# A hybrid block on one core: last accumulators in a bank of their own, a norm's factor left in PSUM, transposes behind the sums, side pairs dealt anew

## The chip, the core and the metric

The kernel runs on one core of a Trainium2 chip. TensorE is called PE here (PEld is its weight load), VectorE DVE, ScalarE ACT, GpSimd POOL and SyncE SP. The metric is the device time of one execution in microseconds (us); a lower one is better.

## What is computed

One layer of a diffusion block on 256 tokens of width 2048, with 256 context tokens, in fp32:

```python
mod = (silu(c) @ ada_w[l] + ada_b[l])
sh1, sc1, g1, sh2, sc2, g2 = jnp.split(mod, N_MOD, axis=-1)
h = modulate(rmsnorm(x, norm1_g[l]), sh1, sc1)
q, k, v, f, hy = split_projection(h @ w_in[l])
kc, vc = jnp.split(hc @ w_in[l][:, NA_WIDTH:3 * NA_WIDTH], 2, axis=-1)
a = neighbourhood_attention(heads(q), heads(k), heads(v), kc_h, vc_h, na_rpb[l])
y = merge_groups(a, fourier_mix(f), hyena_mix(hy, ...), mix_norm_g[l])
x = x + g1 * (y @ w_out[l])
x = x + g2 * conv_gated_mlp(modulate(rmsnorm(x, norm2_g[l]), sh2, sc2), *ffn)
return rmsnorm(x, final_norm_g)
```

`fourier_mix` is a 2-D transform of 4 groups of 128 channels, `hyena_mix` two gated long convolutions of 512 channels. The MLP's inner width is 5632; `split_projection` yields 3 x 1024 columns for attention, 512 for Fourier and 1536 for Hyena.

## The kernel before, in words

**Weights.** Every large product is streamed in chunks of 4 x 128 rows by 512 columns. A chunk is two loads of 512 KB on SP's queue (L268) into a ring of eight buffers `raw`. fp32 precision is had by splitting: ACT casts `raw` to `w_hi` (L173), DVE takes the rest, `w_lo` = `raw` - `w_hi` (L174), and PE makes three products for each tile (hi x hi, lo x hi, hi x lo; L162), 48 matmuls of 128 x 256 for a chunk. `w_hi` and `w_lo` have two buffers each. A chunk's four column tiles nt 0 to 3 of 256 tokens are accumulated in two PSUM banks, two tiles in a bank. The pool `acc_ps` has five banks, `mi_ps` three. In the last chunk of the last column group of w_out and of the down projection the matmuls go tile by tile (`by_nt`), so that nt 3 ends last.

**Side pairs.** The modulation vectors G1, A2, B2 and G2 are dot products that DVE makes: a step (`ada_cols`, L342) loads 512 KB of `ada_col` into the same ring of eight and runs one SCALAR_TENSOR_TENSOR (L351) on it. `pump(n)` (L360) issues 2n such steps. G1, A2 and B2 have 96 steps in all before the FFN, G2 has 32 within it. How many are issued where is set by tables: `p1` gives pairs for each of the five blocks of the kv stage, and `win` gives pairs for each chunk of w_in, added up in `Stream.ready` (L300), which calls `pump(1)` at each whole one. Within an engine the order of instructions is then settled by the scheduler of the tile layer, and `tc.issue_after` puts instructions explicitly behind another.

**Stages.** First the norms, the Hyena filter's spectrum, the modulations and the key and value projections of the context (to about 250 us). Then w_in, 24 chunks, to about 420: chunks 0 to 3 are the Fourier columns, whose sum is copied to `fT` (L737, ACT) and multiplied with a table `fc`; the results are copied to `AB` (L747, L748) and multiplied with `fl`. Chunks 4 to 15 are Hyena's gates and input (`u`, with a width-3 convolution on ACT and DVE, L701 to L703), chunks 16 to 23 the queries. Between them, the two long convolutions: `zt` (L779) times `ftab`, a product with the spectrum on DVE and ACT (L181 to L186), folds on DVE (L792, L795, into `X`), and `X` times `gtab`. Then attention and w_out (16 chunks, to about 551), the second norm, the FFN (557 to 1276) and the end.

**Second norm.** After the last w_out chunk `add_scaled` (L678) adds the four tiles to `xr` on DVE (L681), `square_parts` (L683) squares them on ACT (L694), and `rms_bcast` (L214) sums the squares on PE with a matrix of ones, forms the reciprocal root, spreads it over 128 partitions with four matmuls, copies the result from PSUM to `rb` (L231) and returns it. `modulate` (L250, operation at L252) multiplies each of 16 tiles of `xr` by it and `shift_split` (L254) makes the FFN's `h_hi` on ACT and `h_lo` on DVE. `fill` gives two numbers of matmuls on ones that keep PE at work while it waits.

**End.** `add_scaled` and the squares for the last column group of the down projection, the sums (`col_sums`), the reciprocal root (L985 and `rstd_of`), and the transposition of `xr` to tokens by rows: `turn(n)` makes 8 transposes (L170) for a column group n, `turn(0)` ahead of the sums. Eight tiles of 128 x 512 are scaled by the root, those of tokens 0 to 127 (t = 0) on DVE (L995), those of t = 1 on ACT (L993), and stored from SP's queue, or from ACT's for t = 1 and n > 1 (L996).

## Time and profile before

| what | us |
|---|---|
| runs | 1319.04, 1318.23, 1297.38 (median 1318.23) |
| profiled execution | 1292.37, its span 1290.6 |
| PE busy in the span | 1268.1 (98%) |
| DVE, ACT busy | 889.5 (69%), 555.5 (43%) |
| 200 to 250: PE busy of 50; DMA share, GB/s | 50.00; 0.90, 328 |
| 250 to 260: PE busy of 10; DMA share, GB/s | 10.00; 0.93, 247 |
| 420 to 557: PE busy of 137; DMA share | 135.26; 0.71 |
| mean granted TensorE clock | 0.997 |

Times in the profile run from the start of the span. "Busy" is the time in which an engine has an instruction in work; matmuls overlap, so a busy PE is one that has always something before it, not one at its peak. An average over the span hides the stages: PE's 98% is made of an FFN without a gap and of earlier stretches in which it waits. The DMA share is the mean busy share of the core's 16 DMA engines; near 1, transfers wait for each other. A bracket behind an instruction is its engine's idle time before it, and the instruction or transfer that ended this time.

### The profile page before, as it was taken

To read this page: it belongs to the slowest core of one execution; us is meant where nothing else is said; L and a number is where in the kernel's file an instruction comes from. 1 tells how busy PE (TensorE), PEld (TensorE's weight loads), DVE (VectorE), ACT (ScalarE), POOL (GpSimd) and SP (SyncE) were. 2 spreads that over 40 slices of the span, in tenths; PEclk is the share of its full clock that TensorE was granted. 3 is DMA by queue.
4 is the path that set the end of the run, shared out by engine and by line. 5 is a ranking of instruction groups with operands and counts; after the bars stand their busy time and mean duration, and the time that the engine had idled before them with its cause. 6 is when DMAs were issued, how large, how long until landed. Compare 5 with 4: busy or idle time off the path is not lost.

```text
span 1290.6 us, 24505 instructions
## 1 busy us (share of the span) xinstructions
PE 1268.1 (98%) x10282; PEld 1192.9 (92%) x10282; DVE 889.5 (69%) x1306; ACT 555.5 (43%) x737; POOL 12.0 (1%) x25
## 2 busy tenths in 40 slices
PE   9999999989999999999999999999999999999997
PEld 5768779889899889999999999999999999999997
DVE  5547669968998989987676767744446565655663
ACT  4622212234343665455454545433334444454543
POOL 0000000020000000000000000000000000000000
PEclk9999999999999999999999999999999999999999
DMA  9987878999468855856777777855555656655641
GB/s 365 412 319 288 303 311 306 329 348 323 158 228 325 319 187 173 288 163 222 262 265 257 260 252 263 291 196 196 196 196 183 205 185 199 193 191 191 195 161 66
DMA packets 88399, 315.22 MB, mean 244 GB/s; under 512 B 9952, under 2 KB 10208, under 8 KB 87648
## 3 DMA queue, kind: packets, MB, share of 16 engines
q1 hardware_dynamic: 86944, 311.01, 69.6%
q0 software_dynamic: 768, 1.57, 0.7%
q8 instruction: 80, 1.31, 0.4%
q10 hardware_dynamic: 576, 1.07, 0.2%
q14 instruction: 31, 0.25, 0.1%
HBM read 311.52 MB, written 2.10 MB: 243 GB/s over the span
## 4 chain that ended last, share of the span: by engine, by line
PE 83%; DVE 7%; DMA 6%; ACT 2%; issue 2%; ACTq 0%; DVEq 0%; SPq 0%
PE acc_ps L162 76%; DMA raw<-in_ada_col_t 3%; PE mi_ps L162 3%; DMA raw<-in_w_in_t 3%; PE mi_ps L500 2%; DVE w_lo L174 2%; DVE raw L351 1%; PE mi_ps L170 1%; ACT w_hi L173 1%; DMA pack<-in_pack 0%; DVE Y L788 0%; PE acc_ps L500 0%; DVE bias L658 0%; DVE xr L681 0%; DVE X L795 0%
## 5 line engine op out<-in xcount | busy, mean ns | idle before, releaser
L173 ACT CAST w_hi<-raw 128x1024 fp32r<-128x1024 f32 x376 | 381.3, 1050 | 529.6 <-PE acc_ps L162 444.1
L174 DVE TENSOR_TENSOR w_lo<-raw,w_hi 128x1024 fp32r<-128x1024 f32 x376 | 447.8, 1220 | 221.2 <-ACT w_hi L173 219.9
L162 PE MATMUL acc_ps<-h_hi,w_hi 128*128 128x256 f32 x1408 | 389.0, 277 | 0.5 <-ACT h_hi L256 0.5
L162 PE MATMUL acc_ps<-h_lo,w_hi 128*128 128x256 f32 x1408 | 389.4, 277 | 0.0
L162 PE MATMUL acc_ps<-h_hi,w_lo 128*128 128x256 f32 x1408 | 389.3, 277 | 0.0
L162 PEld LDWEIGHTS acc_ps<-h_hi,w_hi 128*128 128x128 f32 x1408 | 264.2, 188 | 0.6 <-ACT h_hi L256 0.6
L162 PEld LDWEIGHTS acc_ps<-h_hi,w_lo 128*128 128x128 f32 x1408 | 264.5, 188 | 0.0
L162 PEld LDWEIGHTS acc_ps<-h_lo,w_hi 128*128 128x128 f32 x1408 | 264.4, 188 | 0.0
L162 PE MATMUL acc_ps<-yh,w_lo 128*128 128x256 f32 x704 | 194.7, 277 | 0.0
L162 PE MATMUL acc_ps<-yh,w_hi 128*128 128x256 f32 x704 | 194.7, 277 | 0.0
L162 PE MATMUL acc_ps<-yl,w_hi 128*128 128x256 f32 x704 | 194.7, 277 | 0.0
L351 DVE SCALAR_TENSOR_TENSOR raw<-raw,s_row 128x1024 f32<-128x1024 f32 x128 | 154.3, 1218 | 36.4 <-DMA raw<-in_ada_col_t 36.3
L162 PE MATMUL acc_ps<-hx_hi,w_hi 128*128 128x256 f32 x512 | 146.6, 287 | 3.7 <-ACT w_hi L173 3.7
L162 PE MATMUL acc_ps<-hx_hi,w_lo 128*128 128x256 f32 x512 | 143.0, 282 | 1.7 <-DVE w_lo L174 1.7
L162 PE MATMUL acc_ps<-hx_lo,w_hi 128*128 128x256 f32 x512 | 144.0, 282 | 0.0
L162 PEld LDWEIGHTS acc_ps<-yh,w_lo 128*128 128x128 f32 x704 | 132.2, 188 | 0.0
L162 PEld LDWEIGHTS acc_ps<-yh,w_hi 128*128 128x128 f32 x704 | 132.2, 188 | 0.0
L162 PEld LDWEIGHTS acc_ps<-yl,w_hi 128*128 128x128 f32 x704 | 132.2, 188 | 0.0
L162 PEld LDWEIGHTS acc_ps<-hx_hi,w_hi 128*128 128x128 f32 x512 | 97.3, 190 | 9.9 <-ACT w_hi L173 6.8
L162 PEld LDWEIGHTS acc_ps<-hx_lo,w_hi 128*128 128x128 f32 x512 | 97.1, 190 | 2.7 <-issue 2.6
L162 PEld LDWEIGHTS acc_ps<-hx_hi,w_lo 128*128 128x128 f32 x512 | 97.0, 190 | 2.1 <-DVE w_lo L174 2.1
L587 DVE TENSOR_TENSOR kT<-acc_ps,kT 128x512 f32<-128x512 f32 x32 | 22.0, 689 | 28.0 <-PE acc_ps L162 27.9
(245 smaller groups left out, 1530.3 us busy)
## 6 DMA issues: line engine op xcount, KB each, us to landing
raw<-in_ffn_t SPq DMA_DIRECT2D x264, 512.0 KB, 4.3
raw<-in_ada_col_t SPq DMA_DIRECT2D x128, 512.0 KB, 5.2
raw<-in_ada_t SPq DMA_DIRECT2D x64, 512.0 KB, 7.4
raw<-in_w_in_t SPq DMA_DIRECT2D x48, 512.0 KB, 6.5
raw<-in_w_kv_t SPq DMA_DIRECT2D x32, 512.0 KB, 5.8
raw<-in_w_out_t SPq DMA_DIRECT2D x32, 512.0 KB, 4.7
x_in<-in_xT SPq DMA_DIRECT2D x8, 256.0 KB, 5.4
kT<-in_c_tok SPq DMA_DIRECT2D x2, 1024.0 KB, 13.0
```

The costliest lines, as they stand in the source:

```text
L162: return nc.tensor.matmul(ps, lhsT, rhs, start=start, stop=stop, skip_group_check=True)
L170: nc.tensor.transpose(ps, src, ident[:n, :n])
L173: nc.scalar.copy(hi, src)
L174: TT(lo, src, hi.bitcast(F32), op=ALU.subtract)
L351: STT(r, r, 1.0, s_row[:, h * NA : (h + 1) * NA], op0=ALU.mult, op1=ALU.mult, accum_out=sums_[:, f, h : h + 1])
L500: return nc.tensor.matmul(ps[32 * j : 32 * j + 32, :w], s_t[:, kt, :], raws[i // nh][:, kt % nh, :], start=fresh, stop=q == last_q and i i ...
L587: TT(dst, pss[u][:], dst, op=ALU.add)
```

## The change

- `place` puts nt 3 of the last column group of w_out's second half, and of the last group of the down projection, into a third PSUM bank; all else stays two tiles to a bank.
- `rms_bcast` for the second norm returns the PSUM tile itself; the copy at L231 is not made there. Its fill is 6 and 3 for 8 and 5.
- The last three `turn(n)` are issued behind the last matmul of the sums.
- The stores: t = 0 from SP, t = 1 from POOL for n = 0, 1 and from ACT for n = 2, 3.
- `p1` gives 4 and 7 pairs to the third and the last kv block, for 2 and 9 (17 in all as before). `win` gives 0.5 pairs for each of chunks 0 to 3, 1.0 for 4 to 9 and 0.8 for 10 to 23, for 1.5 (0 to 5) and 0.57; 19.2 pairs became 19.26.

```diff
--- before.py
+++ after.py
@@ -44,9 +44,9 @@
 
 CFG = dict(
     ns=2,
-    p1=(0, 0, 2, 6, 9),
+    p1=(0, 0, 4, 6, 7),
     blocks=(2, 2, 4, 4, 4),
-    win=(1.5, 0.57),
+    win=(0.5, 1.0, 0.8),
     att=(1, 0, 1, 4, 0, 1, 0, 0),
     rest=99,
     start='hp pk x0 x1 h3 dc ft a00 a01 a10 a11 W wm si n1s wp n2s q0 f0 ct c0 c1 e e n0 s0 e e h0 w f1 q1 n1 h1 s1',
@@ -211,7 +211,7 @@
             for _ in range(n):
                 mm(ps[:, :P], ones[:], ones[:], True, True)
 
-    def rms_bcast(pool_, sqs, n, name, ps=None, fill=None):
+    def rms_bcast(pool_, sqs, n, name, ps=None, fill=None, keep=True):
         if ps is None:
             ps = bank()
             last = col_sums(ps, sqs)
@@ -227,6 +227,8 @@
             i = mm(ps[:, t * P : (t + 1) * P], ones[:], dg[:], True, True)
         if fill:
             busy(i, fill[1])
+        if not keep:
+            return ps[:, :L]
         rb = pool_.tile([P, L], F32, name=f"{name}_b", tag=f"{name}_b")
         nc.vector.tensor_copy(rb[:], ps[:, :L])
         return rb
@@ -660,14 +662,19 @@
     make_bias()
 
     specs = [(a["w_in_t"], i, 4, 512) for i in range(len(WIN_CHUNKS))]
-    stream = Stream(w1, specs, 1, lambda j: CFG["win"][j > 5])
+    stream = Stream(w1, specs, 1, lambda j: CFG["win"][(j > 3) + (j > 9)])
+
+    def place(pss, nt):
+        if len(pss) == 3 and nt == 3:
+            return pss[2][:, :L]
+        return pss[nt // 2][:, (nt % 2) * L : (nt % 2 + 1) * L]
 
     def wide_chunk(stream, ci, pss, hi_src, lo_src, k0, first, last, by_nt=False):
         wh, wl = stream.get(ci)
         for nt, i in ((nt, i) for nt in range(4) for i in range(4)) if by_nt else ((nt, i) for i in range(4) for nt in range(4)):
-            o = pss[nt // 2][:, (nt % 2) * L : (nt % 2 + 1) * L]
+            o = place(pss, nt)
             ns = slice(nt * P, (nt + 1) * P)
-            mm3(o, wh[:, i, ns], wl[:, i, ns], hi_src[:, k0 + i, :], lo_src[:, k0 + i, :], first and i == 0 and nt % 2 == 0, last and i == 3)
+            mm3(o, wh[:, i, ns], wl[:, i, ns], hi_src[:, k0 + i, :], lo_src[:, k0 + i, :], first and i == 0 and (nt % 2 == 0 or nt == len(pss)), last and i == 3)
 
     def wide(stream, i0, hi_src, lo_src):
         pss = [bank(acc_ps) for _ in range(2)]
@@ -678,7 +685,7 @@
     def add_scaled(pss, n, cols):
         for nt in range(4):
             c = 4 * n + nt
-            STT(xr[:, c, :], pss[nt // 2][:, (nt % 2) * L : (nt % 2 + 1) * L], cols[:, c : c + 1], xr[:, c, :], op0=ALU.mult, op1=ALU.add)
+            STT(xr[:, c, :], place(pss, nt), cols[:, c : c + 1], xr[:, c, :], op0=ALU.mult, op1=ALU.add)
 
     def square_parts(tp, n, parts, tag, bufs):
         sq = tp.tile([P, 4, L], F32, tag=tag, name="sq4", bufs=bufs)
@@ -859,7 +866,7 @@
         def wout_chunk(h, n, kc):
             yh, yl = ((yB_hi, yB_lo), (yA_hi, yA_lo))[h]
             if kc == 0:
-                held[n] = [bank(acc_ps) for _ in range(2)]
+                held[n] = [bank(acc_ps) for _ in range(2 + (h == 1 and n == 3))]
             wide_chunk(stream, h * 8 + n * 2 + kc, held[n], yh, yl, kc * 4, kc == 0, kc == 1, h * kc == 1 and n == 3)
             if kc == 1:
                 add_scaled(held[n], n, G1)
@@ -901,12 +908,12 @@
             for kc in range(2):
                 wout_chunk(1, n, kc)
         pump(CFG["rest"])
-        rb2 = rms_bcast(ap_, x_parts, D, "r2", fill=(8, 5))
+        rb2 = rms_bcast(ap_, x_parts, D, "r2", fill=(6, 3), keep=False)
         STT(A2[:], A2[:], 1.0, vec[:, V_N2 : V_N2 + KT], op0=ALU.add, op1=ALU.mult)
         h2_hi = rtile("C", [P, KT, L], F32R, "h2_hi")
         h2_lo = rtile("D", [P, KT, L], F32R, "h2_lo")
         for k in range(KT):
-            t = modulate(ap_, xr[:, k, :], A2[:, k : k + 1], rb2[:])
+            t = modulate(ap_, xr[:, k, :], A2[:, k : k + 1], rb2)
             shift_split(t, B2[:, k : k + 1], h2_hi[:, k, :], h2_lo[:, k, :])
     mids.close()
     fp = pool(ctx, "ffn", 1, "right")
@@ -956,7 +963,7 @@
                 pump(99)
             gs = halves[g]
             for n in range(4):
-                pss = [bank(acc_ps) for _ in range(2)]
+                pss = [bank(acc_ps) for _ in range(2 + (g == 1 and n == 3))]
                 for q in gs:
                     wide_chunk(stream, ci, pss, *ys[q], 0, q == gs[0], q == gs[-1], g == 1 and n == 3 and q == gs[-1])
                     ci += 1
@@ -980,12 +987,13 @@
 
     sums = bank()
     turn(0)
-    col_sums(sums, f_parts)
+    summed = col_sums(sums, f_parts)
     ms = fp.tile([P, 2], F32, name="rf_m")
     TS(ms[:], sums[:, 0:2], 1.0 / D, EPS, op0=ALU.mult, op1=ALU.add)
     r = rstd_of(fp, ms[:], 2, "rf")
-    for n in range(1, 4):
-        turn(n)
+    with tc.issue_after(summed.ins):
+        for n in range(1, 4):
+            turn(n)
     for n in range(4):
         for t in range(2):
             z = slice(n * 512, (n + 1) * 512)
@@ -993,7 +1001,7 @@
                 nc.scalar.activation(o_tok[:, t, z], turned[t, n][:], AF.Copy, scale=r[:, t : t + 1])
             else:
                 TS(o_tok[:, t, z], turned[t, n][:], r[:, t : t + 1], None, op0=ALU.mult)
-            (nc.scalar if t and n > 1 else nc.sync).dma_start(out[t * P : (t + 1) * P, z], o_tok[:, t, z])
+            (nc.sync if not t else nc.scalar if n > 1 else nc.gpsimd).dma_start(out[t * P : (t + 1) * P, z], o_tok[:, t, z])
 
 
 def laid_out(inp):
```

Three places where instructions stand differently. The first is SP's queue at the start of w_in, from the first load of chunk 0; `ada_col_t` are the side steps. Before:

```order
L268 DMA raw<-in_w_in_t 128x1024 x2
L268 DMA raw<-in_ada_col_t 128x1024 x2
L268 DMA raw<-in_w_in_t 128x1024 x2
L268 DMA raw<-in_ada_col_t 128x1024 x4
L732 DMA fc<-in_fou_c 128x128
L733 DMA fl<-in_fou_l 128x2x512
```

After that, two or four side steps stand behind each of chunks 2 to 5. With the change:

```order
L270 DMA raw<-in_w_in_t 128x1024 x4
L270 DMA raw<-in_ada_col_t 128x1024 x2
L270 DMA raw<-in_w_in_t 128x1024 x4
L739 DMA fc<-in_fou_c 128x128
L740 DMA fl<-in_fou_l 128x2x512
```

Chunks 0 and 1 follow each other, and 2 and 3; the side steps stand behind them, and later, where before two chunks followed each other, there are two steps behind nearly every chunk. On ACT at the same place, the casts (`w_hi_2686` before and `w_hi_2662` now are chunk 4, `w_hi_2806` now is chunk 5) and the copies of the Fourier sum. Before:

```order
L173 CAST w_hi_2686<-raw_2682 128x1024
L737 COPY fT_2459<-acc_ps_2460 128x512
L737 COPY fT_2459<-acc_ps_2461 128x512
L173 CAST w_hi_2686<-raw_2684 128x1024
L747 COPY AB_2748<-mi_ps_2752 128x256
```

With the change:

```order
L173 CAST w_hi_2662<-raw_2658 128x1024
L173 CAST w_hi_2662<-raw_2660 128x1024
L744 COPY fT_2459<-acc_ps_2460 128x512
L173 CAST w_hi_2806<-raw_2802 128x1024
L744 COPY fT_2459<-acc_ps_2461 128x512
L173 CAST w_hi_2806<-raw_2804 128x1024
```

The second copy of `fT` has moved behind the first cast of chunk 5; on PE the first matmuls on `fT` now stand directly behind chunk 3's last, where four of chunk 4's stood between.

The second place is PE at the second long convolution: the last weight matmuls before the first product with `gtab`. Before (`w_hi_3749` is chunk 17, `w_hi_3807` chunk 18):

```order
L162 MATMUL acc_ps_3744<-hx_hi_89,w_lo_3750 128x256
L162 MATMUL acc_ps_3743<-hx_hi_89,w_hi_3807 128x256
L162 MATMUL acc_ps_3743<-hx_lo_1394,w_hi_3807 128x256
L162 MATMUL acc_ps_3744<-hx_hi_89,w_hi_3807 128x256
L162 MATMUL acc_ps_3744<-hx_lo_1394,w_hi_3807 128x256
L162 MATMUL mi_ps_3721<-gtab_99,X_3693 128x128
```

With the change (`w_hi_3735` is chunk 17):

```order
L162 MATMUL acc_ps_3730<-hx_hi_89,w_lo_3736 128x256
L162 MATMUL acc_ps_3729<-hx_hi_89,w_hi_3735 128x256
L162 MATMUL acc_ps_3729<-hx_lo_903,w_hi_3735 128x256
L162 MATMUL acc_ps_3730<-hx_hi_89,w_hi_3735 128x256
L162 MATMUL acc_ps_3730<-hx_lo_903,w_hi_3735 128x256
L162 MATMUL mi_ps_3707<-gtab_99,X_3679 128x128
```

From the last product with `ftab` to the first with `gtab` the order holds 82 weight matmuls before and 62 now.

The third place is PE at the end, after the last matmul of the down projection. Before:

```order
L170 MATMUL mi_ps<-pack,xr 128x128 x8
L162 MATMUL mi_ps<-ones,part 128x1 x2
L162 MATMUL mi_ps<-ones,sq_13996 128x1 x4
L170 MATMUL acc_ps<-pack,xr 128x128
L162 MATMUL mi_ps<-ones,sq_13996 128x1 x2
L170 MATMUL acc_ps<-pack,xr 128x128 x6
L162 MATMUL mi_ps<-ones,sq_13996 128x1 x2
L170 MATMUL acc_ps<-pack,xr 128x128 x13
L170 MATMUL mi_ps<-pack,xr 128x128 x4
```

With the change:

```order
L170 MATMUL mi_ps<-pack,xr 128x128 x8
L162 MATMUL mi_ps<-ones,part 128x1 x2
L162 MATMUL mi_ps<-ones,sq_13992 128x1 x8
L170 MATMUL acc_ps<-pack,xr 128x128 x20
L170 MATMUL mi_ps<-pack,xr 128x128 x4
```

The seven transposes that stood between the sums are behind them. On SP four stores remain of six, and POOL has two. At the second norm ACT's order was two squares, a cast, two squares, a cast; it is now three squares, a cast, one square, a cast.

## The prediction

> **What bounds the kernel now.** I read the table of busy time by stage first. Its columns after the stretch are its length and the busy time (with the count) of PE, PEld, DVE, ACT and POOL, then the granted TensorE clock, the share of the DMA engines and GB/s.
>
> ```profile
> 260.00:310.00 50.00, 45.93 (x369) 44.52 (x368) 37.24 (x57) 21.25 (x29) 8.47 (x13) 1.00 1.03 346
> 310.00:320.00 10.00, 8.22 (x58) 8.05 (x57) 8.21 (x14) 3.63 (x5) 0.00 (x0) 0.83 0.93 325
> 320.00:370.00 50.00, 48.07 (x389) 45.16 (x387) 48.56 (x71) 20.02 (x28) 0.00 (x0) 1.00 0.64 221
> 370.00:420.00 50.00, 49.34 (x398) 46.64 (x399) 46.12 (x70) 18.77 (x22) 0.00 (x0) 1.00 0.68 249
> 557.00:1276.00 719.00, 718.54 (x6338) 718.32 (x6337) 441.95 (x527) 325.96 (x386) 0.00 (x0) 1.00 0.64 210
> ```
>
> Three things are to be seen. The FFN (last row) is PE without a gap: 718.54 us for 6338 matmuls, 0.113 us each, and nothing in the change takes a matmul from it. Between 260 and 320 us the transfers are the limit: their share is 1.03 and 0.93, PE stands 4.07 + 1.78 = 5.85 us and runs at a clock of 0.83 for 10 us, which costs another 1.7 us. Between 320 and 420 DVE is full (48.56 and 46.12 of 50) while the transfers have room.
>
> The chain of what ended last says the same: loads of 11 us there, and one piece of PE to the end of the FFN.
>
> ```profile
> 264.32 11.28 DMA raw<-in_w_in_t
> 299.42 10.84 DMA raw<-in_ada_col_t
> 557.96 718.56 PE acc_ps L162 x6336
> ```
>
> Then the timeline, for the waits inside that stretch (the bracket is PE's idle time and what ended it):
>
> ```profile
> 268.19 0.39 PE L162 MATMUL acc_ps<-hx_hi,w_lo 128*128 128x256 f32 x1 [0.75 <-DVE w_lo L174]
> 276.80 0.39 PE L162 MATMUL acc_ps<-hx_hi,w_hi 128*128 128x256 f32 x1 [3.11 <-ACT w_hi L173]
> 312.13 0.48 PE L170 MATMUL mi_ps<-pack,u 128*128 128x128 f32 x2 [1.78 <-DVE u L703]
> 313.15 0.41 PE L162 MATMUL acc_ps<-hx_hi,w_hi 128*128 128x256 f32 x1
> 316.35 0.38 PE L162 MATMUL acc_ps<-hx_hi,w_hi 128*128 128x256 f32 x1
> 317.15 0.28 PE L162 MATMUL acc_ps<-hx_hi,w_lo 128*128 128x256 f32 x1
> 275.70 1.04 ACT L173 CAST w_hi<-raw 128x1024 fp32r<-128x1024 f32 x1 [7.03 <-DMA raw<-in_w_in_t]
> 276.65 1.07 ACT L737 COPY fT<-acc_ps 128x512 f32<-128x512 f32 x2
> ```
>
> 0.75 + 3.11 + 1.78 = 5.64 of the 5.85 us are three waits; in the second, PE waits for a split that itself waited 7.03 us for a load. A matmul takes 0.41 us at 313.15 (and so up to 316.35), and 0.28 again at 317.15: that is the low clock behind the third wait. The 3.11 us wait was followed by no such stretch.
>
> **The change, part by part.** The sum is made against the profiled execution, 1292.4 us (span 1290.6 and 1.8 around it). It lies 25.9 us below the median of the three runs shown, 1318.2 (1297.4 to 1319.0), and 5 below the fastest; what the change is worth should be the same in each, the level of a measurement need not be.
>
> *Side pairs.* The multiset of loads and multiplications stays; 17 pairs are dealt over the kv blocks as before, and 19.3 in place of 19.2 over the w_in chunks. By the order, before the split of chunk 0 as many side steps stand as before (34); by chunks 4 to 6 there are six fewer (40 for 46, 42 for 48, 46 for 52), and the last are back by chunks 22 and 23. Six steps are 3 MB of 512 KB loads: 9 us at the 346 GB/s of the first row. So the loads of chunks 4 and 5 stand that much earlier in the queue, and the 0.75 and 3.11 us waits go; the third, on a gate of DVE (L703) held up by a side load, goes with the same relief, and so does the low clock that followed it. What comes in their place: behind chunk 3 the order now has the Fourier copies around a cast on ACT (CAST of chunk 4, copy fT, CAST of chunk 5's first half, copy fT), and the PE matmuls on fT directly behind chunk 3. Copy, cast, copy are 0.53 + 1.04 + 0.53 = 2.1 us from the ACT rows; PE has at most ten matmuls beside them, so I count the 2.1 in full, and 0.2 us of small waits stays. Gain: 7.6 - 2.1 - 0.2 = **5.3 us**. Bounds: 7.6 (all goes) and 0 (chunk 5 is late in the way chunk 4 was).
>
> The price stands between 360 and 385 us, where the second long convolution's transform waits for DVE:
>
> ```profile
> 370.01 3.70 PE L162 MATMUL mi_ps<-zt,ftab 128*128 128x512 f32 x8 [0.42 <-ACT zt L779]
> 382.39 2.48 DVE L795 TENSOR_TENSOR X<-Y 128x512 f32<-128x512 f32 x4
> 383.12 4.30 PE L162 MATMUL mi_ps<-gtab,X 128*128 128x128 f32 x32
> ```
>
> Before, PE bridges the chain zt, X, gtab with 82 weight matmuls, 9.3 us, and just reaches gtab as X is ready. By the order the change leaves 62: 20 fewer, 20 x 0.113 = 2.3 us in which PE would stand if the chain on DVE takes as long as before. It will take no less, since side steps come back here at 0.8 pairs a chunk for 0.57:
>
> ```profile
> L351 DVE SCALAR_TENSOR_TENSOR raw<-raw,s_row 128x1024 f32<-128x1024 f32 x128 | 154.3, 1218 | 36.4 <-DMA raw<-in_ada_col_t 36.3
> ```
>
> From chunk 16 to 20 that is about one pair more in five chunks, 2.4 us of DVE, of which a third would fall into this chain: 0.8. Loss **3.1 us**; bounds 0 (fewer splits ahead of the chain, so it ends sooner) and 4.7 (2.3 + both steps). The pairs dealt earlier in the kv blocks (4 for 2 in the third, 7 for 9 in the last) cost nothing: the order has as many steps before w_in as before, and the transfers and DVE in the third block have room; bounds 1 either way.
>
> *Second norm.* Now the stages around the FFN's start:
>
> ```profile
> 550.85 0.81 ACT L694 ACTIVATE sq<-xr 128x256 f32<-128x256 f32 x2 [2.88 <-DVE xr L681]
> 551.49 0.88 DVE L681 SCALAR_TENSOR_TENSOR xr<-acc_ps,G,xr 128x256 f32<-128x256 f32 x2 [0.28 <-PE acc_ps L162]
> 551.56 1.03 ACT L173 CAST w_hi<-raw 128x1024 fp32r<-128x1024 f32 x1
> 552.50 0.71 ACT L694 ACTIVATE sq<-xr 128x256 f32<-128x256 f32 x2
> 556.42 0.42 DVE L231 COPY r_b<-mi_ps 128x256 f32<-128x256 f32 x1 [0.67 <-PE mi_ps L162]
> 556.88 0.88 DVE L252 SCALAR_TENSOR_TENSOR ht<-xr,A,r_b 128x256 f32<-128x256 f32 x2
> 557.96 0.61 PE L162 MATMUL acc_ps<-h_hi,w_hi 128*128 128x256 f32 x3 [0.46 <-ACT h_hi L256]
> ```
>
> The copy goes and ht starts in its place: 556.88 - 556.42 = 0.46 us on the chain to the first FFN matmul. Reading the factor from PSUM is counted as nothing: L681, with an operand in PSUM, takes 0.44 as L252 does. The third bank lets nt 2 be added 0.3 us sooner, but the order on ACT then is three squares, the cast, the last square: that one starts behind 551.66 + 0.4 + 1.03 = 553.1 and ends near 553.5, where the last of before ends at 553.2. So 0.46 less 0.25, with a shorter fill worth up to 0.1: gain **0.3 us** (-0.1 to 0.6).
>
> *End.* The rows of the last norm:
>
> ```profile
> 1276.56 0.88 DVE L681 SCALAR_TENSOR_TENSOR xr<-acc_ps,G,xr 128x256 f32<-128x256 f32 x2 [1.85 <-PE acc_ps L162]
> 1277.60 1.03 PE L162 MATMUL mi_ps<-ones,sq 128*128 128x1 f32 x8
> 1278.49 0.31 PE L170 MATMUL acc_ps<-pack,xr 128*128 128x128 f32 x1
> 1278.64 0.50 PE L162 MATMUL mi_ps<-ones,sq 128*128 128x1 f32 x4
> 1279.00 0.85 PE L170 MATMUL acc_ps<-pack,xr 128*128 128x128 f32 x6
> 1279.69 0.50 PE L162 MATMUL mi_ps<-ones,sq 128*128 128x1 f32 x4
> 1280.23 0.16 DVE L985 TENSOR_SCALAR rf_m<-mi_ps 128x2 f32<-128x2 f32 x1 [2.80 <-PE mi_ps L162]
> 1282.50 4.05 SPq L996 DMA_DIRECT2D out<-o_tok  x6
> ```
>
> Seven transposes stand between the sums: 1278.64 - 1278.49 = 0.15 and 1279.69 - 1279.00 = 0.69. Behind them now, they bring rf_m and all that follows **0.8 us** forward. The third bank makes the last squares ready earlier, but PE is busy with eight transposes and the first sums until 1278.5, so it adds nothing. The moved transposes (24 at 0.12 us) end before ACT and DVE ask for them. Then the output, 2.1 MB in eight tiles:
>
> ```profile
> GB/s 0 0 0 0 0 0 0 0 0 0 0 0 0 0 0 0 0 0 0 21 0 221 404 415 399 373 405 368 320 394 415 399 410 410 362 105 0 0 0 0
> out<-o_tok SPq DMA_DIRECT2D x6, 256.0 KB, 3.4
> out<-o_tok ACTq DMA_DIRECT2D x2, 256.0 KB, 3.6
> bias<-in_na_rpb POOLq DMA_DIRECT2D x16, 96.0 KB, 6.5
> ```
>
> The first row is the rate in 40 slices of 0.39 us from 1275.0: some 400 GB/s without a break until 1289, so issuing faster buys little, and starting sooner buys what the start moves. Two tiles leave from POOL, whose only transfers of before, of 96 KB, took 6.5 us to land where SP's took 3.4. They are issued by my timing at 1281.7 and 1282.4; the second lands at 1288.9, just with the rest. I keep 0.8; bounds 1.6 (the start moves by as much again, since SP's first tile is no longer one of ACT's, for which it waited until 1282.50) and -2.0 (9.5 us for these larger tiles).
>
> The Trainium skill speaks of that path: "DMA: Bandwidth & Descriptors", section "Anatomy of one DMA — SWDGE (gpsimd) path", gives about 2.0 us plus bytes over 436 GB/s, an estimate of 2.6 us for 256 KB. The 6.5 us row of a third of the size does not agree; by the page POOL's tiles could not be last, and the end would gain up to 1.6. Its section "Issuing engines are not separate DMA queues" speaks against gaining more than issue time.
>
> Sum: -5.3 + 3.1 - 0.3 - 0.8 = -3.3, so 1292.4 - 3.3 = **1289 us**.
>
> **The rivals.** *The chain moves with its cover (1286).* Fewer splits stand ahead of X on DVE, so gtab's 2.3 + 0.8 us come to nothing: 1292.4 - 6.4. For it: in the row 320:370 DVE has 48.56 of 50 filled with work that partly goes ahead of X. Against: X still needs the folds and the ACT copies, which no table shortens. *Slower: chunk 5 comes late (1294.4).* The copy of fT's second half now stands behind chunk 5's cast on ACT. Its load takes the slot that chunk 3's split frees, near 264, where before's load of chunk 4 was issued (264.32 in the chain); PE has done chunk 3's last 46 matmuls near 272.5 (268.19 + 46 x 0.113, less the wait of 0.75). From a load of 8.5 us on PE waits, and at the 11.28 us of the chain's row it stands 2.8 us and has lost what it saved by the time of the copies; the gain of 5.3 goes and the 3.1 stays: 1292.4 + 3.1 - 1.1 = 1294.4. For it: the row 264.32. Against: the six loads fewer in front of it. *POOL's tiles land last (1292).* At 9.5 us, half as long again as its row, the end loses 2.0 for a gain of 0.8: 1289.1 + 2.8 = 1291.9. For it: 6.5 us at 96 KB. Against: part of this time is likely the queue of other loads, which stands empty at the end.
>
> The Trainium skill's "TensorE: Matmul & The Clock Gate", section "Part 1: The HAM clock gate (the "warmup" mystery)", has the clock watched by a free-running window of some 3.4 us. The trace agrees in the length (313.15 to about 316.5) and in that a longer wait, 3.11 us, went free. By that rule any wait that is left could cost another 1.7 us by its phase alone.
>
> **How the numbers follow.** Forecast 0.55, full relief 0.2, late chunk 0.15, POOL last 0.1. The forecast's own range is 1284 (7.6 gained, nothing lost) to 1294 (2 gained, 4.7 lost); the rivals lie in it or at its edge. The range is 1283 to 1316: its lower end is full relief with every other bound good (1292.4 - 7.6 - 0.6 - 1.6 = 1282.6), its upper end holds a measurement at the level of the shown median (1318.2 less 3). A measurement of this kernel tells about 2% from no change, 26 us; no case reaches that by its sum. The shown runs' own spread of 1.7% leaves 0.1 for faster and 0.04 for slower, and 0.86 for no difference.
>
> **What would show it.** Right: between 260 and 320 PE idle near 3 us (5.85 before) and a clock of 1.00; PE waiting 2 to 3 us for X L795 before the second gtab; no copy of r_b and the first FFN matmul 0.3 us sooner behind the last w_out matmul; rf_m 0.8 us sooner behind the last FFN matmul; outputs of POOL landing with those of SP. Wrong: an idle PE behind the fT copies longer than 2.5 us, no wait at gtab, or a last output that comes from POOL. The FFN must stay at 718.5 us; if it moves, the reason lies outside of this sum.

## The result, and the profile after

Over 22 executions of each, the changed kernel takes 1.007 times the kernel before, with an interval of 1.0052 to 1.0088: 9 us **slower** (7 to 11), where 3 us faster was forecast. In some executions, seen in the profiles of eight kernels below, with and without the edits, the FFN alone takes 746 us in place of 718; the comparisons leave such executions out, the medians (1304.6 after, 1319.0 before) and the profiles' spans do not.

The profiled execution of the changed kernel has a span of 1311.4 us. Its last matmul of w_out starts at 562.43 us, in the kernel before at 551.17: 11.3 us are lost up to there. (Its FFN took 728.7 us; with the same code in the FFN behind_split and keep_win below have 718.1 and 718.3, so these 10 us are not the change's.) The table by stage, with the columns of the prediction's first fence:

```profile
260.00:310.00 50.00, 40.23 (x286) 39.02 (x286) 28.31 (x44) 15.32 (x22) 9.13 (x14) 0.86 0.97 268
310.00:320.00 10.00, 9.98 (x86) 9.81 (x84) 8.13 (x14) 4.00 (x6) 0.00 (x0) 1.00 0.98 335
320.00:370.00 50.00, 48.55 (x387) 45.58 (x387) 48.64 (x70) 19.39 (x26) 0.00 (x0) 1.00 0.60 199
370.00:420.00 50.00, 46.02 (x363) 43.49 (x362) 48.24 (x76) 19.17 (x25) 0.00 (x0) 0.97 0.73 272
```

Between 260 and 310 PE now stands 9.8 us where it stood 4.1, and DVE works 28 of 50 us where it worked 37, with 268 GB/s for 346. The DMA share stays near 1 (0.97 for 1.03) though the rate falls by a fifth, so that share alone doesn't tell that no more could be moved. Between 370 and 420 PE stands 4.0 us where it stood 0.7. The clock, in slices of 5 us:

```profile
270.00:275.00 5.00, 4.74 (x29) 4.74 (x30) 4.86 (x7) 0.00 (x0) 1.30 (x2) 0.69 0.92 238
295.00:300.00 5.00, 2.97 (x14) 3.00 (x15) 2.62 (x5) 3.13 (x5) 0.92 (x2) 0.50 0.89 203
300.00:305.00 5.00, 5.00 (x30) 5.00 (x30) 4.88 (x12) 0.24 (x1) 1.30 (x2) 0.62 1.01 161
```

PE's busy time in these slices at the lost share of the clock is 4.74 x 0.31 + 2.97 x 0.50 + 5.00 x 0.38 = 4.9 us more. The three waits that carry the loss, on PE, and what DVE did before the first two:

```profile
270.26 0.58 PE L162 MATMUL acc_ps<-hx_hi,w_lo 128*128 128x256 f32 x1 [2.56 <-DVE w_lo L174]
297.03 1.84 PE L162 MATMUL mi_ps<-ones,sqf 128*128 128x1 f32 x8 [7.21 <-DVE sqf L724]
391.55 2.76 PE L162 MATMUL mi_ps<-gtab,X 128*128 128x128 f32 x14 [3.98 <-DVE X L802]
```

```profile
267.84 1.23 DVE L353 SCALAR_TENSOR_TENSOR raw<-raw,s_row 128x1024 f32<-128x1024 f32 x1 [4.63 <-DMA raw<-in_ada_col_t]
268.99 2.36 DVE L174 TENSOR_TENSOR w_lo<-raw,w_hi 128x1024 fp32r<-128x1024 f32 x2
...
291.49 1.23 DVE L353 SCALAR_TENSOR_TENSOR raw<-raw,s_row 128x1024 f32<-128x1024 f32 x1 [3.77 <-DMA raw<-in_ada_col_t]
292.64 1.28 DVE L772 TENSOR_TENSOR fo<-mi_ps,fq 128x512 f32<-128x512 f32 x2
295.04 1.23 DVE L353 SCALAR_TENSOR_TENSOR raw<-raw,s_row 128x1024 f32<-128x1024 f32 x1 [1.12 <-DMA raw<-in_ada_col_t]
296.19 0.69 DVE L724 TENSOR_TENSOR sqf<-sqf 128x512 f32<-128x512 f32 x1
```

This is the reading on which the rest depends. DVE **idles** for 4.63 us, released by the load of a side step, and behind that side multiplication stands the low split of chunk 3, whose two loads and casts were done by 264.0. (Rows of 0.08 us, in which DVE reads out a sum, are left out above.) The same at 291.49: the Fourier result `fo` stands behind a side multiplication of a load that came late, and `sqf` behind the next. PE waits for w_lo and for sqf, and what keeps it is the transfer in front of them. On the page the group of side multiplications has this row (36.4 before, in the prediction):

```profile
L353 DVE SCALAR_TENSOR_TENSOR raw<-raw,s_row 128x1024 f32<-128x1024 f32 x128 | 154.7, 1220 | 54.0 <-DMA raw<-in_ada_col_t 53.7
```

The chunks' own loads are no longer late, as forecast: ACT's casts of chunks 2 and 3 now wait for PE to give a buffer back, where before the cast of chunk 4 waited for its load.

```profile
256.52 2.00 ACT L173 CAST w_hi<-raw 128x1024 fp32r<-128x1024 f32 x2 [3.35 <-PE acc_ps L162]
261.96 2.01 ACT L173 CAST w_hi<-raw 128x1024 fp32r<-128x1024 f32 x2 [3.44 <-PE acc_ps L162]
```

The other edits, at the second norm and at the end:

```profile
568.71 0.74 PE L162 MATMUL acc_ps<-h_hi,w_hi 128*128 128x256 f32 x4 [0.45 <-ACT h_hi L258]
1297.44 0.28 PE L162 MATMUL acc_ps<-yh,w_lo 128*128 128x256 f32 x1
1300.77 0.16 DVE L992 TENSOR_SCALAR rf_m<-mi_ps 128x2 f32<-128x2 f32 x1 [2.52 <-PE mi_ps L162]
```

```profile
out<-o_tok SPq DMA_DIRECT2D x4, 256.0 KB, 3.8
out<-o_tok POOLq DMA_DIRECT2D x2, 256.0 KB, 3.8
out<-o_tok ACTq DMA_DIRECT2D x2, 256.0 KB, 4.1
```

From the last w_out matmul to the first of the FFN 6.28 us (6.79 before); from the last FFN matmul to rf_m 3.32 (3.99), to the end of the span 13.96 (14.35). POOL's stores land as fast as SP's.

### The profile page after: what moved, and what is told of

Same layout as the page of the kernel before. It is cut to its first block, busy times and chain, and to the rows that moved or that the text cites. A ratio compares the mean times of both kernels' runs of the same rounds, so it can differ in the third digit from the quotient of the medians.

```text
span 1311.4 us, 24482 instructions
## 1 busy us (share of the span) xinstructions
PE 1282.3 (98%) x10274; PEld 1203.5 (92%) x10274; DVE 887.7 (68%) x1305; ACT 554.3 (42%) x737; POOL 13.2 (1%) x27
## 4 chain that ended last, share of the span: by engine, by line
PE 84%; DVE 7%; DMA 5%; issue 1%; ACT 1%; DVEq 0%; ACTq 0%; SPq 0%
PE acc_ps L162 78%; DMA raw<-in_ada_col_t 5%; PE mi_ps L162 3%; DVE w_lo L174 2%; PE mi_ps L502 2%; PE mi_ps L170 1%; DVE raw L353 1%; ACT w_hi L173 1%; DMA pack<-in_pack 0%; DVE Y L795 0%; DMA raw<-in_ffn_t 0%; PE acc_ps L502 0%; DVE bias L660 0%; DVE xr L688 0%; DVE X L802 0%
## 5 line engine op out<-in xcount | busy, mean ns | idle before, releaser
L162 PEld LDWEIGHTS acc_ps<-h_hi,w_lo 128*128 128x128 f32 x1408 | 267.4, 190 | 0.5 <-DVE w_lo L174 0.5
L162 PEld LDWEIGHTS acc_ps<-h_hi,w_hi 128*128 128x128 f32 x1408 | 264.0, 188 | 0.6 <-ACT h_hi L258 0.6
L353 DVE SCALAR_TENSOR_TENSOR raw<-raw,s_row 128x1024 f32<-128x1024 f32 x128 | 154.7, 1220 | 54.0 <-DMA raw<-in_ada_col_t 53.7
L708 ACT ACTIVATE ga<-acc_ps,pack 128x256 f32<-128x256 f32 x44 | 23.7, 559 | 38.3 <-PE acc_ps L162 32.8
```

Source lines behind the costliest of these rows:

```text
L162: return nc.tensor.matmul(ps, lhsT, rhs, start=start, stop=stop, skip_group_check=True)
L353: STT(r, r, 1.0, s_row[:, h * NA : (h + 1) * NA], op0=ALU.mult, op1=ALU.mult, accum_out=sums_[:, f, h : h + 1])
L708: nc.scalar.activation(dst, ps, AF.Identity, bias=b, scale=w1_)
```

## The experiments

**Theory**: the deal of side pairs is the loss. DVE takes its instructions in order. With fewer side steps ahead of them the chunks' loads come early, but in the built order side multiplications now stand on DVE ahead of a split and of the Fourier result, soon after their own loads were issued; DVE waits there for these loads, and PE behind it. A second, smaller part is the shorter cover of the second transform. **Rivals**: the other edits (A); p1 (B); transfers that are too slow in any order (C).

In the table, "w_out" is the start of the last w_out matmul in the profile. It sums up all that happens before the FFN, and it scatters: the kernel before, old_deal and old_deal_sp have the same tables and 551.2, 550.8 and 547.2; keep_win and keep_win_sp have 549.7 and 555.1. Differences under some 5 us are not read from it. "c3", "sqf" and "gtab" are PE's idle times (us) before chunk 3's first low part, the Fourier sums and the second gtab product; a dash is none over 0.5. "side" is DVE's idle time that side loads ended (us), "PE, clk" the busy time of 50 and the clock between 260 and 310.

| kernel | ratio to before (interval) | w_out | PE, clk | c3 | sqf | gtab | side |
|---|---|---|---|---|---|---|---|
| before | 1 | 551.2 | 45.9, 1.00 | 0.75 | - | - | 36.3 |
| changed | 1.007 (1.0052 to 1.0088) | 562.4 | 40.2, 0.86 | 2.56 | 7.21 | 3.98 | 53.7 |
| old_deal | 1.0003 (0.9986 to 1.002) | 550.8 | 45.9, 1.00 | as before | - | - | 35.2 |
| new_win | 1.0086 (1.006 to 1.0113) | 564.5 | 38.4, 0.86 | - | 11.64 | 3.59 | 55.5 |
| new_p1 | 1.003 (0.9985 to 1.0075) | 547.0 | 45.5, 1.00 | as before | - | - | 32.6 |
| keep_win | 1.0002 (0.9972 to 1.0032) | 549.7 | 45.9, 0.97 | as before | - | - | 35.4 |
| behind_split | no interval; 1292.1 and 1292.2 | 551.9 | 49.9, 1.00 | - | - | 2.61 | 35.3 |
| hold6 | 1.0052 (1.0025 to 1.0078) | 559.8 | 42.7, 0.90 | - | 7.27 | 3.58 | 46.0 |
| behind_fo | 1.0016 (0.9995 to 1.0037) | 556.5 | 45.1, 0.97 | 1.19 | - | 3.51 | 51.1 |
| both_holds | no interval | 555.9 | 46.9, 1.00 | - | - | 2.77 | 39.9 |
| hold_c10 | 1.0024 (0.9997 to 1.0051) | 553.4 | 49.6, 1.00 | - | - | - | 36.2 |
| hold_old | 1.0006 (0.9958 to 1.0053) | 550.1 | 45.9, 1.00 | as before | - | - | 34.3 |

**Which part: old_deal, new_win, new_p1, keep_win.** old_deal is the changed kernel with both tables as before:

```diff
-    p1=(0, 0, 4, 6, 7),
+    p1=(0, 0, 2, 6, 9),
-    win=(0.5, 1.0, 0.8),
+    win=(1.5, 0.57),
```

(and the index of `win` with it). Expected:

> The changed kernel with both tables of side pairs as before (p1 and win); the third bank, the factor in PSUM, the moved transposes and the POOL stores stay. Theory (the loss is in the new deal: on DVE, which works in order, side multiplications stand ahead of weight splits and of the Fourier result and wait there for their own late loads; PE waits behind): about 1 us faster than before, ratio 0.999, since the changed kernel's own profile has 0.5 us less at the second norm and 0.4 us less at the end. DVE's wait for side loads as in the profile before, 36 us (54 in the changed kernel). Rival A (the loss comes from the other edits, a reordering by the scheduler or the POOL stores): as slow as the changed kernel, ratio 1.007.

new_win is the kernel before with only the new `win`, new_p1 the kernel before with only the new `p1`:

```diff
-    win=(1.5, 0.57),
+    win=(0.5, 1.0, 0.8),
```

> The kernel before with the new win table alone (0.5, 1.0, 0.8 pairs a chunk). Theory: the whole loss, 8 to 10 us slower than before (ratio 1.007), with PE waits near 2.7 us at chunk 3 and 7 us at the Fourier sums, and DVE waiting some 50 us for side loads. Rival A (other edits): within 1 us of before. Rival B (the kv stage's new p1 brings the loads out of step): within 2 us of before.

```diff
-    p1=(0, 0, 2, 6, 9),
+    p1=(0, 0, 4, 6, 7),
```

> The kernel before with the new p1 table alone (4 and 7 pairs for 2 and 9 in the third and the last kv block). Theory: within 2 us of before, ratio 0.999 to 1.002; the start of w_in no more than 1.5 us later. Rival B (p1 brings the loads out of step): 6 us slower or more, with the waits of the changed kernel in the Fourier stretch.

`win` alone brings the whole loss (1.0086), and without it there is none (1.0003): rival A falls. Where the loss shows is not fixed: in new_win the wait at chunk 3 is missing and the one at the Fourier sums is longer, 11.64 us, so my numbers for the two were wrong singly and near in sum (10 expected). new_p1's ratio decides nothing by its interval; its profile has none of the changed kernel's waits. keep_win puts it to the test with the other edits in place (`p1` new, `win` old):

> The changed kernel with win as before (1.5, 0.57) and p1 as changed. Theory: the whole loss hangs on win, so this one is as old_deal, ratio 0.996 to 1.001 to before; 82 matmuls cover the second transform. Rival B (p1 brings the loads out of step): ratio 1.003 or more.

1.0002: p1 has no part that shows, to within the interval's 0.3% (4 us), and this profile has none of the changed kernel's waits. So rival B falls.

**By which way: behind_split.** The changed kernel with one ordering added, and no load, table or count touched: in the w_in stage a side multiplication stands on DVE behind the low split of the chunk after which it was dealt.

```diff
-                        pump(1)
+                        pump(1, self.w.last if self.hold else None)
...
-                STT(r, r, 1.0, s_row[:, h * NA : (h + 1) * NA], op0=ALU.mult, op1=ALU.mult, accum_out=sums_[:, f, h : h + 1])
+                with tc.issue_after(after.ins) if after else nullcontext():
+                    STT(r, r, 1.0, s_row[:, h * NA : (h + 1) * NA], op0=ALU.mult, op1=ALU.mult, accum_out=sums_[:, f, h : h + 1])
```

> The changed kernel with one thing added: in the w_in stage each side multiplication stands on DVE behind the low split of the chunk after which its load was issued. No load, no count and no table is changed. Theory (place on DVE decides): the 2.7 us wait at chunk 3 goes, the 7.4 us wait at the Fourier sums shrinks below 2, and the kernel comes within 2 us of before, on either side. Rival C (the transfers are too slow in this stretch whatever the order, 268 GB/s for 346): no more than 2 us better than the changed kernel, since PE then waits for the chunks' own loads, whose ring buffers come free later.

The stretch is full, PE 49.88 of 50 us (45.93 before), at 298 GB/s:

```profile
260.00:310.00 50.00, 49.88 (x403) 48.51 (x402) 39.16 (x61) 21.50 (x30) 7.82 (x12) 1.00 1.00 298
```

In its DVE timeline the side multiplications no longer wait:

```profile
261.85 2.36 DVE L174 TENSOR_TENSOR w_lo<-raw,w_hi 128x1024 fp32r<-128x1024 f32 x2 [3.08 <-ACT w_hi L173]
264.13 1.22 DVE L354 SCALAR_TENSOR_TENSOR raw<-raw,s_row 128x1024 f32<-128x1024 f32 x1
...
280.33 1.29 DVE L773 TENSOR_TENSOR fo<-mi_ps,fq 128x512 f32<-128x512 f32 x2 [2.12 <-PE mi_ps L162]
```

`fo` now waits for PE and comes 12 us sooner than at 292.64. The same loads in the same order on SP now move at 298 GB/s for 268 and PE does not wait for them, so rival C falls. The kernel is at the level of before (two times of 1292.1 and 1292.2; span 1290.3), and not below it, since waits of 2.09 us at 315 (for the copy `zt` on ACT), 2.55 at 341 and 2.61 before gtab came behind it, each with a lower clock beside it (0.66, 0.81 and 0.66 in the slices of 5 us from 315, 340 and 380).

**The two places apart: hold6 and behind_fo.** hold6 applies the edge of behind_split to chunks 0 to 5 only, and in behind_fo all side multiplications dealt from chunk 5 on stand behind `fo`, with nothing held behind a split.

```diff
-                        pump(1, self.w.last if self.hold else None)
+                        pump(1, self.w.last if self.hold and j < 6 else None)
```

> As behind_split, but side multiplications are held behind their chunk's split for chunks 0 to 5 only; in the order 62 weight matmuls stand before the second product with gtab, as in the changed kernel (82 in the kernel before). Theory (two separate losses, the Fourier stretch and the cover of the second transform): between 260 and 310 PE is busy over 48 us of 50 and its clock is 1.00, while the wait before gtab stays at 3 to 4.5 us; in all within 3 us of before. Rival D (one cause: the late side loads delay the X chain too, and with the Fourier stretch mended the gtab wait goes as well): no wait before gtab over 1 us.

```diff
-                        pump(1, self.w.last if self.hold else None)
+                        pump(1, made_fo[-1] if self.hold and made_fo else None)
```

> The changed kernel, with the side multiplications that are dealt behind the Fourier part (from chunk 5 on) put behind the Fourier result fo on DVE; nothing is held behind a split. In the order one side multiplication of chunk 4 still stands ahead of chunk 3's low split. Theory: the counterpart to hold6: the wait of 2 to 3 us at chunk 3 stays, and the 7.4 us wait before the Fourier sums is gone (under 1 us), with the low clock behind it. Rival F (the Fourier result is late for another reason than the side multiplications ahead of it, its matmuls or copies): the wait stays above 4 us.

In hold6 the wait at chunk 3 is gone, and that at the sums is still there, to my surprise: the two side multiplications of chunk 6 stand ahead of `fo`, and one of chunk 7 ahead of `sqf`, beyond the edge. So it is 0.5% slower than before and not within the 3 us expected.

```profile
282.29 1.23 DVE L354 SCALAR_TENSOR_TENSOR raw<-raw,s_row 128x1024 f32<-128x1024 f32 x1 [4.15 <-DMA raw<-in_ada_col_t]
283.45 1.23 DVE L354 SCALAR_TENSOR_TENSOR raw<-raw,s_row 128x1024 f32<-128x1024 f32 x1
284.61 1.28 DVE L773 TENSOR_TENSOR fo<-mi_ps,fq 128x512 f32<-128x512 f32 x2
289.36 1.23 DVE L354 SCALAR_TENSOR_TENSOR raw<-raw,s_row 128x1024 f32<-128x1024 f32 x1 [3.47 <-DMA raw<-in_ada_col_t]
```

In behind_fo it is the reverse: 1.19 us at chunk 3 (2 to 3 were expected) and no wait at the sums. Rival F falls. But the next link, the reciprocal root of the group norm, now stands between side multiplications that wait for their loads, and PE waits 3.53 us for it:

```profile
293.11 1.23 DVE L356 SCALAR_TENSOR_TENSOR raw<-raw,s_row 128x1024 f32<-128x1024 f32 x1 [1.57 <-DMA raw<-in_ada_col_t]
294.26 0.16 DVE L195 SCALAR_TENSOR_TENSOR gn_s<-gn_r,gn_m 128x2 f32<-128x2 f32 x1
296.90 1.23 DVE L356 SCALAR_TENSOR_TENSOR raw<-raw,s_row 128x1024 f32<-128x1024 f32 x1 [2.48 <-DMA raw<-in_ada_col_t]
298.05 0.16 DVE L196 TENSOR_TENSOR gn_s<-gn_s,gn_r 128x2 f32<-128x2 f32 x1
```

In both the wait before gtab stays at 3.5 us. That of hold6 says little on rival D (one cause for all), as the Fourier wait is still there; that of behind_fo, and the 2.61 us of behind_split, speak against it. But the cover alone isn't the cause either: it is 62 weight matmuls in hold6 and 76 in behind_fo, with the same wait. both_holds joins the two edges, holding chunks 0 to 5 behind their split and later ones behind `fo`:

> Both edges: side multiplications of chunks 0 to 5 behind their chunk's split, and those from chunk 5 on behind fo. Theory: both waits go, PE busy over 49 of 50 between 260 and 310 at a clock of 1.00; 76 weight matmuls cover the second transform (62 in the changed kernel, 82 before), so up to 2 us of wait before gtab stays; ratio 0.997 to 1.001 to before. Rival C (transfers too slow in any order): waits for the chunks' own loads of 5 us and more between 260 and 320.

Neither wait is left, but PE is busy 46.9 us of 50, not 49, with 1.09 us before `fT`, 1.30 before the group norm's factor and 4.07 at `u` near 310. It has no ratio of its own. The wait before gtab is 2.77 us, above the "up to 2" expected, and rival D falls by it: both Fourier waits are mended and it stays.

What it is made of can be read from the traces: the time from the start of the second transform's products with `ftab` to its first with `gtab`, and the cover in between. In the changed kernel DVE runs a side multiplication just ahead of this chain's first step:

```profile
376.82 3.70 PE L162 MATMUL mi_ps<-zt,ftab 128*128 128x512 f32 x8
378.29 1.21 DVE L353 SCALAR_TENSOR_TENSOR raw<-raw,s_row 128x1024 f32<-128x1024 f32 x1
380.61 0.68 DVE L184 TENSOR_TENSOR X<-mi_ps,Y 128x512 f32<-128x512 f32 x1
```

From 376.82 to 391.55 are 14.73 us; before, from 370.01 to 383.12, it was 13.11, as in every kernel with 82 or 83 matmuls of cover (13.11 to 13.13). So 3.98 us is 20 matmuls less, 20 x 0.113 = 2.3 us, and a chain longer by 1.6. With 62 or 63 matmuls the others have chains of 14.33 us and waits of 3.2 to 3.6; with 76, six less, behind_split, both_holds and behind_fo have chains of 14.94, 15.32 and 16.05 and waits of 2.61, 2.77 and 3.51. There the longer chain is most of the wait.

**Is there a better kernel: hold_c10, holds_750, holds_1000, hold_old.** With the orders held, `win` was set so that both transforms keep their cover:

```diff
-    win=(0.5, 1.0, 0.8),
+    win=(0.5, 1.2, 0.6),
```

> The changed kernel with win = (0.5, 1.2, 0.6) and side multiplications held behind their chunk's split for chunks 0 to 9; in the order 81 and 82 weight matmuls stand before the two products with gtab (81 and 62 in the changed kernel). Theory: both losses go, PE busy over 48 of 50 between 260 and 310, no wait over 1 us before gtab, and the kernel is 4 to 7 us faster than before, ratio 0.995 to 0.997. Rival D agrees on the first and not on the cause of the second; rival C (transfers too slow in any order): within 2 us of before.

Each wait that I meant to take away is away, and the kernel is no faster (1.0024). New ones stand behind: 3.27 us for the copy `zt`, which on ACT stands behind two casts of later chunks; 2.68 at a split near 344; and 10.7 us from the last w_out matmul to the FFN, 6.8 before, since this table deals 17.6 pairs and the rest came at the end, which I had not counted.

```profile
316.89 1.59 PE L162 MATMUL mi_ps<-zt,ftab 128*128 128x512 f32 x3 [3.27 <-ACT zt L787]
```

holds_750 (both edges, `win` 0.75, 1.2, 0.65) and holds_1000 (1.0, 1.0, 0.66) deal all pairs:

> Both edges, the hold for all chunks, and win = (0.75, 1.2, 0.65), 19.3 pairs as before; 81 and 83 weight matmuls cover the two transforms. Theory: no wait over 1 us in the Fourier stretch nor before either gtab; what is left are waits where ACT's casts stand ahead of the copies of zt (2 to 3.5 us at 313 in hold_c10 and behind_split). 3 to 6 us faster than before, ratio 0.9955 to 0.998.

> As holds_750 with win = (1.0, 1.0, 0.66), 19.2 pairs, two steps more before the Fourier result; 83 and 82 matmuls cover the transforms. Theory: the same, 2 to 5 us faster than before; if loads of chunk 4 come late again as in the kernel before (3.1 us), it is 3 us behind holds_750.

holds_750 had a ratio of 1.0112 with an interval of 0.9967 to 1.0256, holds_1000 1.0026 (0.9997 to 1.0055), and their last w_out matmuls are at 556.6 and 556.8: no gain shows. In holds_750 my prediction's rival came true, the copy of `fT` behind the cast of chunk 5, whose load is late, and PE waits 2.85 us for it:

```profile
276.05 1.04 ACT L173 CAST w_hi<-raw 128x1024 fp32r<-128x1024 f32 x1 [3.19 <-DMA raw<-in_w_in_t]
277.00 0.58 ACT L747 COPY fT<-acc_ps 128x512 f32<-128x512 f32 x1
```

hold_old has the old tables with the hold:

> The changed kernel's other edits with the old tables, and all side multiplications of w_in held behind their chunk's split. Theory: the old deal's waits are for the chunks' own loads (3.1 us at chunk 4), which no place on DVE shortens, so the 0.75 and 3.1 us waits stay: within 3 us of before. Rival E (it is the hold alone that gains, the tables do not matter): as fast as hold_c10, 4 us or more below before.

It is as before (1.0006), a wait of 2.96 us at chunk 4 included: the hold does not shorten it where the chunk's own load is the late one. Nothing speaks for rival E, though the interval (0.9958 to 1.0053) is too wide to exclude its 4 us.

**Late load or busy DVE: pair_late.**

```diff
+                loaded.append((mult, r))
...
+        while len(loaded) > (0 if n >= 99 else 2):
+            f, r = loaded.pop(0)
+            f(r)
```

> The changed kernel with every side pair's two multiplications issued one pair later than its two loads; tables, loads and counts stay, and the two transforms keep 81 and 63 weight matmuls of cover (81 and 62). Theory (it is the late load that holds DVE, not the 1.2 us of the multiplication): DVE's wait for side loads falls from 54 to under 30 us, the waits of 2.7 and 7.4 us shrink below 1.5 each, the wait before gtab of 3 to 4 us stays; 4 to 8 us faster than the changed kernel, ratio to before 0.999 to 1.004. Rival G (the place and the busy time of the multiplications decide, not their loads): the Fourier wait stays above 5 us. A risk to both: two ring buffers more are held, so chunk loads may come late in their place.

This one tells nothing on its question. In its trace the side multiplications of the Fourier stretch stand where they stood, ahead of the same splits and of `fo` and `sqf`: the order that was built did not follow the program's. It shows the same waits, 2.15, 5.82 and 3.20 us, side loads hold DVE 54.1 us, and its ratio is 1.0076 (1.0037 to 1.0115): a repetition of the changed kernel. That the load and not the work holds DVE rests on the brackets above and on DVE's 28 busy us of 50, and rival G has no experiment of its own.

**The stores: old_deal_sp and keep_win_sp**, with stores from SP and ACT as in the kernel before:

```diff
-            (nc.sync if not t else nc.scalar if n > 1 else nc.gpsimd).dma_start(out[t * P : (t + 1) * P, z], o_tok[:, t, z])
+            (nc.scalar if t and n > 1 else nc.sync).dma_start(out[t * P : (t + 1) * P, z], o_tok[:, t, z])
```

> old_deal with the eight stores from the queues of the kernel before (six from SP, two from ACT). From the last FFN matmul to the end of the span the kernel before takes 14.35 us, old_deal 14.07. If the POOL stores land late (my rival of the prediction), this one ends 0.5 us or more sooner than old_deal, near 13.5; if they only save issue time, it ends between 14.0 and 14.4.

> keep_win with all stores as in the kernel before (SP and ACT). From old_deal_sp, the end is 13.3 us behind the last FFN matmul where POOL stores gave 13.6 to 14.2: 0.3 to 0.9 us faster than keep_win, too little for the ratio, seen in the profile's end. If the end takes 14 us or more, that one look was scatter.

From the last FFN matmul to the end: 13.26 us in old_deal_sp against 14.07 in old_deal, but 13.82 in keep_win_sp against 13.86 in keep_win (ratio 1.0007, 0.9982 to 1.0032). The 13.26 us was scatter; the stores cost and gain nothing that shows.

## Why the prediction was wrong

- **What bounds the stretch**: half right. Before, loads ended the longest wait, but I took "fewer loads ahead" for "no wait". The step that failed is "So the loads of chunks 4 and 5 stand that much earlier in the queue, and the 0.75 and 3.11 us waits go", with all that may come in their place put at 2.1 us for the `fT` copies and 0.2 us of small waits; waits for side loads on the way were put at nothing.

  The chunks' loads did come earlier and the 3.11 us wait went; the one of 0.75, at chunk 3, grew to 2.56, one of 7.21 came at the sums, and the `fT` copies, which I had counted in full, cost PE no wait of 0.3 us or more. I counted how many side steps stand ahead of each split and did not read on DVE which ones, nor how soon after its issue DVE comes to each side load.

  DVE came to the load that held chunk 3's split 4.4 us after its issue (9.0 with the wait) and to the one ahead of `fo` 6.0 us after (9.8 with the wait); they took 8.9 and 9.7 us to land. In the kernel before those used between 263 and 290 took longer, 10.1 to 13.8 us, but DVE came to them 10.6 to 14.0 us after their issue and waited 0.3 us at most. So it is not that the loads had become slower. The order showed it: one side multiplication of chunk 4 ahead of chunk 3's split.

  By idle time and clock (the clock in slices of 5 us) the stretch 260 to 320 costs 9.8 + 4.9 = 14.7 us, against 5.9 + 1.4 = 7.3 before (the clock there 3.22 x 0.19 + 5.00 x 0.16, where the prediction had 1.7): +7.4 in place of -5.3.
- **The price at the second transform**: the mechanism was right, the size 3.1 near: 3.98 us of wait where 0.1 stood, and some 1.4 us of low clock behind it (0.97 over 50 us). The 2.3 us of cover were right; the 0.8 us of longer chain measured 1.6, of which the side multiplication at 378.29 is 1.2. From 320 to 420 PE's idle time and the clock make 4.0 + 1.5 + 1.4 us, against 0.7 + 1.9 before: +4.3, and 7.4 + 4.3 = 11.7 is near the 11.3 us lost up to the last w_out matmul.
- **p1**: right, nothing that shows (keep_win, 1.0002). The totals of `win` were the wrong way round in my text: 19.26 pairs became 19.2, and both deal 19 whole pairs.
- **Second norm**: 0.5 for a forecast 0.3. Over all profiles with this code the time there goes with the clock: 5.9 to 6.3 us in the six that keep a clock of 1.00, 6.4 to 7.1 in the seven in which it falls (0.89 over 550 to 565 in old_deal and keep_win), hold_c10 with its late pairs left aside. Without the edit and at a clock of 1.00 it is 6.8 (before) and 6.7 (new_p1). So the edit is worth 0.4 to 0.9 us, and the low clock often takes it back. Whether the shorter fill brings on the low clock is open.
- **End**: rf_m comes 0.67 us sooner in every kernel with the edit (3.32 for 3.99), 0.8 was forecast; of it 0.4 reaches the end in the changed kernel. POOL's 3.8 us was far from the bound of 9.5 that I took from its 6.5 us row.
- **The rivals**: "slower" had 0.15, by chunk 5's load. It was the side loads. That the late load could be one that nobody but DVE's queue waits for was the case missing from the list.

The trace also bears on the rule of the Trainium skill that the prediction weighed ("TensorE: Matmul & The Clock Gate", "Part 1: The HAM clock gate (the "warmup" mystery)"): the clock falls after an idle window of some 3.4 us. It agrees in part: the 7.21 us wait goes with slices of 0.50 and 0.62, and the 3.98 us wait with a stage mean of 0.97. But the clock was low beside shorter waits too, of 2.56 us here (0.69) and 1.78 before (0.83), and not beside one of 3.11 before, so the length of a wait alone does not tell. And the Trainium skill's estimate of 2.6 us for POOL's stores ("DMA: Bandwidth & Descriptors", "Anatomy of one DMA — SWDGE (gpsimd) path") was nearer to the 3.8 us measured than the 6.5 us row. It is for one transfer; here eight stores were under way together, and those from SP took 3.8 us too.

Open is what a deal with the long distance of the old table and the early chunk loads of the new would bring; none of the tables tried has both.

## What to carry to other kernels

When loads are dealt anew, look on the engine that uses them at how soon after its issue the engine comes to each one, against the time that such a load takes to land, and at what stands behind it in that engine's order: a transfer off the critical path is on it as soon as an instruction of the path queues behind its user. The queue that was freed for the chunks' loads bought nothing here, since DVE then came to the side loads before they had landed. And a wait can be paid twice, once idle and once at the low clock: here those of 1.78, 2.56, 3.98 and 7.21 us were, and the one of 3.11 us was not.

## What was not expected

Mending waits one by one moved them on: with each edge taken, another link of the same chain (sqf, the group norm's factor, `u`, `zt`) was found behind a side multiplication or a cast, and of the six repaired kernels that have a ratio all but hold6 lie within 0.3% of the kernel before or have an interval that holds it. And a change of program order, as in pair_late, may leave the order on an engine as it was: only the built order tells.
